# Decoder block on one core: a fixed order of three engines up to the first feature product, twelve warm products ahead of it, and a first weight chunk of four tiles

## The chip, the core and the metric

The kernel runs on one core of one Trainium2 chip. The metric is the device time of one execution in microseconds (us). The engines are PE (matrix products), DVE (VectorE), ACT (ScalarE), POOL (GpSimd) and SP, whose queue issues the loads.

## The reference, cut to what matters

One layer of a decoder runs on 256 prompt tokens and 8 x 4 sample tokens, 288 columns in all, with 2048 features. Its beginning is what the change touches:

```python
mod = silu(c) @ w_ada + b_ada                 # conditioning, 6 parts of 2048
sh1, sc1, g1, sh2, sc2, g2 = split(mod, 6)
h = rmsnorm(x, norm1) * (1 + sc1) + sh1       # modulated input
proj = h @ w_in                               # feature products
u_pool, z, xbc, dt_raw = split(proj, ...)
```

After it come the pooling mixer, the state-space mixer, the output projection, a gated feed-forward network and a last norm. All data is fp32, and the time is spent on products of weights that are streamed once from HBM.

## The kernel before, in words

The features lie on partitions: `xa` holds x as 16 blocks of 128 features by 288 columns. A **feature product** of fp32 accuracy is made of three PE products in the function `mm3` (lines 229 to 231): the weight is split into a rounded high half `whi` (a cast on ACT, L223) and a rest `wlo` (a subtraction on DVE, L224), the modulated input h likewise into `h1h` (ACT, L375) and `h1l` (DVE, L376), and PE adds whi\*h1h, whi\*h1l and wlo\*h1h.

The first projection (tiles called `xbc`) has 28 output tiles of 128 features. It doesn't wait for all of the conditioning: the 16 blocks of h are taken in six groups, `KGROUPS` = 1, 1, 2, 4, 4, 4 blocks. For each group, `ada_group_units` makes the conditioning of its blocks on PE (`adag`, L308), copies it out on ACT (`asb`, L263), turns it with a product (`adat`, L323), and adds the bias on DVE (`ada`, L333; `amul`, L275). `modulate` then makes h: a product with the reciprocal norm (L363), scale and shift of the prompt columns (L366), scale and shift of the sample columns (L372, L373), and the split (L375, L376). For group 0 the sample columns are done on DVE, for the others on POOL. Then `xbc_units` runs the 28 tiles of the group: group 0 copies its results from PSUM to SBUF alternately on ACT and DVE (L589), later groups add theirs on DVE (L591).

The weights come in pieces of 512 KB into 16 buffers (`raw`), issued by SP in the order of the program: four conditioning pieces of group 0, the chunks of group 0's weights, four conditioning pieces of group 1, and so on. `_xbc_chunks` cuts a group's weights into chunks of 1024 columns: in group 0, 8 tiles each and 4 in the last. There are two buffers each for `whi` and `wlo`. A planner orders the instructions of each engine by program order and by when it expects their inputs, so they needn't run in the order in which they are written.

The conditioning of later groups is mixed into the tiles of the group at hand: the generator `nxt` is pulled once after each tile listed in `AT` (for groups 0 and 1) or at the rate `AR` (from group 2). Four pulls load a batch of four pieces, and the next pull runs the products of this batch (in group 1's case also its modulation) and starts the next load. `AN` = 4 pulls are made ahead of group 0.

**Warm products** (`warm_pe`, L179) are 128 x 128 products whose result nobody reads. `WU` says how many: 14 at the start, 2 after each block of squares, 2 after each of the first two conditioning pieces, and 2 after group 0's `adat`.

The norm runs ahead of that: squares of x on ACT and DVE (L427, L429), their sums on PE (`ssum`, L431, and `ssum1b`, L191), a square root on ACT (L197), a reciprocal on DVE (L198), and a broadcast on PE (`pbrstd`, L202).

Of the kernel before, what the change touches and what calls it, by code (L numbers as in the profile page):

```python
# [36 lines left out]
EPS = 1e-6  # L37
WU = (14, 2, 2, 2, 2)
RAW0, RAW1, RAW2 = 8, 8, 1
# [5 lines left out]

AT = ([16, 18, 20, 22], [0, 1, 2, 3, 8, 10, 12, 18, 20, 22, 24, 26])
AR = (0, 0, 0.43, 0.62, 0.62)
# [89 lines left out]
def kernel(ctx: ExitStack, tc, ins, outs):  # L137
# [34 lines left out]
    nc.scalar.activation(sc_c[:, :, 0:NC9], ct, AF.Silu)  # L172

    wps = aux("warm")

# [17 lines left out]

    def rstd_of(ps, n, name, keep=True):
# [3 lines left out]
        nc.vector.reciprocal(r3, r3)  # L198
        pb = aux("pb" + name)
# [13 lines left out]
    def load(key):  # L213
# [3 lines left out]
        return t  # L217

    def split(raw, a, n, name, urgent=True):
        hi = wp[0].tile([P, RAWC], F32R, tag="whi", name="whi_" + name)  # L220
        lo = wp[0].tile([P, RAWC], F32R, tag="wlo", name="wlo_" + name)
        with tc.high_priority() if urgent else nullcontext():
            nc.scalar.copy(hi[:, :n], raw[:, a:a + n])  # L223
            nc.vector.tensor_tensor(lo[:, :n], raw[:, a:a + n], hi[:, :n].bitcast(F32), ALU.subtract)  # L224
        return hi, lo

# [33 lines left out]

    def ada_sb(ps, nb, name, r=P, pin=False):
        asb = kp.tile([P, 512], F32, tag="asb", name="asb_" + name)
        i = nc.scalar.copy(asb[0:r, :nb], ps[0:r, :nb])  # L263
        if pin:
            tc.keep_in_program_order(i)
        return asb
# [13 lines left out]
    def ada_group_units(gi):  # L280
# [7 lines left out]
        kstep = 2 if gk == 1 else 1  # L288
        begun = False
        first = True  # L290
        for q0 in range(0, nq, AQ[gi]):
            raws = []
            for q in range(q0, min(q0 + AQ[gi], nq)):
                raws.append((q, load(("ada", gi, q))))
                yield

            for q, raw in raws[::-1] if gi else raws:
                for kk in range(0, per, kstep):
                    k = q * per + kk
                    for j in range(nj if gk > 1 else 4):  # L300
                        if gk == 1:

                            ck, c = k + j // 2, kk * 256 + j * P
                        else:
                            ck, c = k, kk * nj * nb + j * nb
                        left = q0 + AQ[gi] >= nq and q == raws[0 if gi else -1][0] and kk + kstep >= per
                        with tc.high_priority() if begun else nullcontext():
                            i = nc.tensor.matmul(ps[32 * j:32 * j + 32, :nb], sc_c[:, ck, :], raw[:, c:c + nb],  # L308
                                                 start=first, stop=left, tile_position=(0, 32 * j))
                        if begun:  # L310
                            tc.keep_in_program_order(i)
                        begun = gi > 0
                    first = False
                if gi == 0 and q < WU[3]:
                    warm_pe(WU[2], raw[:, 0:P])
            begun = False
        r = 32 * nj
        if gi == 0:
            ready["xbc", 0, 0] = split(load(("xbc", 0, 0)), 0, RAWC, "xbc0_0")
        if gk == 1:  # L320
            asb = ada_sb(ps, nb, f"g{gi}", pin=gi == 0)
            pt = aux(f"adat_g{gi}")
            nc.tensor.matmul(pt[:, :r], asb[:, :nb], early[:, K_S2:K_S2 + r], start=True, stop=True)  # L323
            if gi == 0:
                warm_pe(WU[4], asb[:, 0:P])
        else:
            pt = ada_tr(ada_sb(ps, nb, f"g{gi}", r), nb, f"g{gi}", r)
# [30 lines left out]

    def modulate(xv, rstd, which, shp, k0, gk, name, eng=None):

        h = kp.tile([P, 4, N], F32, tag="hmod", name="h_" + name, bufs=2)
        hv = h[:, :gk, :]
        nc.vector.tensor_tensor(hv, xv,  # L363
                                rstd.unsqueeze(1).to_broadcast([P, gk, N]), ALU.mult)
        for i in range(gk):
            nc.vector.tensor_scalar(h[:, i, 0:NP], h[:, i, 0:NP], amul[:, which, k0 + i, 0:1],  # L366
                                    ada[:, shp, k0 + i, 0:1], ALU.mult, ALU.add)
# [4 lines left out]
        eng.tensor_tensor(hs, hs, sa, ALU.mult)  # L372
        eng.tensor_tensor(hs, hs, sb, ALU.add)  # L373
        for i in range(gk):
            nc.scalar.copy(xhi[0][k0 + i], h[:, i, :])  # L375
            nc.vector.tensor_tensor(xlo[0][k0 + i], h[:, i, :], xhi[0][k0 + i].bitcast(F32), ALU.subtract)  # L376
# [42 lines left out]


    nc.scalar.activation(warm, sc_c[:, 0, 0:1], AF.Sqrt, scale=0.0)
    warm_pe(WU[0])
    ssum = aux("ssum1")
    for q in range(4):
        sq = kp.tile([P, 4, N], F32, tag="hmod", name=f"sq{q}", bufs=2)
        if q % 2 == 0:
            nc.scalar.activation(sq, xa[q], AF.Square)  # L427
        else:
            nc.vector.tensor_tensor(sq, xa[q], xa[q], ALU.mult)  # L429
        for i in range(4):  # L430
            nc.tensor.matmul(ssum[32 * i:32 * i + 32, :N], ones[:, 0:32], sq[:, i, :],  # L431
                             start=(q == 0), stop=(q == 3), tile_position=(0, 32 * i))
        warm_pe(WU[1], sq[:, 0, 0:P])
    sqs = kp.tile([P, N], F32, tag="xsq", name="sqs", bufs=2)
    nc.vector.tensor_copy(sqs, ssum[:, :N])
    ssum = aux("ssum1b")
    col_sums(ssum, sqs, early[:, K_S4:K_S4 + 1], True, True)
    rstd1p, rstd1 = rstd_of(ssum, D, "rstd1")

# [879 lines left out]
```

## Time and profile before

| | |
|---|---|
| median of 3 runs | 1378.33 us (1378.28 to 1380.17) |
| profiled execution | 1378.2 us, of which its span (first to last instruction) 1376.3 us |
| PE busy in the span | 1354.7 us |
| DVE, ACT, POOL busy | 824.3, 570.2, 223.6 us |
| read from HBM | 309.78 MB |

The span is what the trace shows; 1.9 us of the execution lie around it. Times in the trace count from the span's start.

### The profile page before, as it was taken

The page shows a single profiled execution, that of the slowest core. Times are in us where ns is not written, and L with a number is a line of the kernel's source. Part 1 is how long each engine was busy: PE and PEld are TensorE (multiplying, and loading weights), DVE is VectorE, ACT ScalarE, POOL GpSimd, SP SyncE. Part 2 cuts the span into 40 slices and gives each one's busy share as a digit, 9 for nine tenths or more (in the row PEclk, how much of TensorE's full clock was granted, in tenths as well). Part 3 has the DMA queues.
Part 4 walks back from the last instruction along what each step waited for, and adds up shares of the span by engine and source line. Part 5 has one row for each costly group of instructions (what it writes and reads, how often), then busy time and mean ns, then how long its engine had stood idle before and what let it go on. Part 6 is the DMA issues. An engine that isn't in the chain of part 4 may idle for free.

```text
span 1376.3 us, 26243 instructions
## 1 busy us (share of the span) xinstructions
PE 1354.7 (98%) x10557; PEld 1254.3 (91%) x10557; DVE 824.3 (60%) x1376; ACT 570.2 (41%) x889; POOL 223.6 (16%) x430
## 2 busy tenths in 40 slices
PE   8999999999999999999999999999999999999997
PEld 7788987776779898989999999999999999999997
DVE  4875658977674348644665445666565556566553
ACT  4223224478553334533433333443433334443452
POOL 0000001212122213111221001212120012132221
PEclk9999999999999999999999999999999999999998
DMA  9987766988887878778555555555555555555531
GB/s 380 408 347 274 303 229 242 341 295 297 306 338 291 322 256 278 236 271 296 190 179 182 170 168 188 201 183 188 187 173 163 183 198 181 196 191 192 184 119 70
DMA packets 97194, 323.20 MB, mean 235 GB/s; under 512 B 10736, under 2 KB 19888, under 8 KB 97072
## 3 DMA queue, kind: packets, MB, share of 16 engines
q1 hardware_dynamic: 93168, 310.63, 63.8%
q0 software_dynamic: 3184, 9.69, 1.9%
q8 instruction: 83, 1.36, 0.4%
q10 hardware_dynamic: 720, 1.19, 0.2%
q14 instruction: 39, 0.32, 0.1%
HBM read 309.78 MB, written 10.39 MB: 233 GB/s over the span
## 4 chain that ended last, share of the span: by engine, by line
PE 94%; DVE 4%; DMA 1%; ACT 1%; issue 0%; POOL 0%; DVEq 0%; POOLq 0%; ACTq 0%
PE mm_down L231 7%; PE mm_down L229 7%; PE mm_down L230 7%; PE mm_gate L231 6%; PE mm_gate L229 6%; PE mm_val L230 6%; PE mm_gate L230 6%; PE mm_val L231 6%; PE mm_val L229 6%; PE adap L258 4%; PE xbc L229 4%; PE xbc L231 4%; PE xbc L230 4%; PE mm_out L229 3%; PE mm_out L230 2%; PE mm_out L231 2%
## 5 line engine op out<-in xcount | busy, mean ns | idle before, releaser
L229 PE MATMUL mm_down<-ah,whi_down 128*128 128x288 f32 x688 | 203.7, 296 | 0.0
L231 PE MATMUL mm_down<-ah,wlo_down 128*128 128x288 f32 x688 | 203.5, 296 | 0.0
L230 PE MATMUL mm_down<-al,whi_down 128*128 128x288 f32 x688 | 203.3, 295 | 0.0
L231 PE MATMUL mm_gate<-h2h,wlo_gate 128*128 128x288 f32 x640 | 190.2, 297 | 0.0
L229 PE MATMUL mm_gate<-h2h,whi_gate 128*128 128x288 f32 x640 | 189.8, 297 | 0.0
L230 PE MATMUL mm_gate<-h2l,whi_gate 128*128 128x288 f32 x640 | 189.3, 296 | 0.0
L230 PE MATMUL mm_val<-h2l,whi_val 128*128 128x288 f32 x640 | 188.8, 295 | 0.0
L231 PE MATMUL mm_val<-h2h,wlo_val 128*128 128x288 f32 x640 | 188.5, 295 | 0.0
L229 PE MATMUL mm_val<-h2h,whi_val 128*128 128x288 f32 x640 | 188.0, 294 | 0.0
L224 DVE TENSOR_TENSOR wlo_gate<-raw_gate,whi_gate 128x1024 fp32r<-128x1024 f32 x80 | 98.0, 1226 | 139.1 <-ACT whi_gate L223 139.0
L224 DVE TENSOR_TENSOR wlo_down<-raw_down,whi_down 128x1024 fp32r<-128x1024 f32 x96 | 107.5, 1120 | 116.7 <-ACT whi_down L223 115.2
L223 ACT CAST whi_down<-raw_down 128x1024 fp32r<-128x1024 f32 x96 | 92.2, 961 | 168.9 <-PE mm_down L230 120.6
L223 ACT CAST whi_gate<-raw_gate 128x1024 fp32r<-128x1024 f32 x80 | 83.9, 1050 | 163.7 <-PE mm_gate L230 71.8
L229 PE MATMUL xbc<-h1h,whi_xbc 128*128 128x288 f32 x448 | 136.0, 305 | 4.3 <-ACT h1h L375 2.3
L223 ACT CAST whi_val<-raw_val 128x1024 fp32r<-128x1024 f32 x80 | 84.1, 1051 | 123.9 <-issue 100.2
L231 PE MATMUL xbc<-h1h,wlo_xbc 128*128 128x288 f32 x448 | 131.5, 301 | 2.2 <-DVE wlo_xbc L224 2.0
L230 PE MATMUL xbc<-h1l,whi_xbc 128*128 128x288 f32 x448 | 132.7, 297 | 0.0
L230 PEld LDWEIGHTS mm_down<-al,whi_down 128*128 128x128 f32 x688 | 129.7, 189 | 0.0
L231 PEld LDWEIGHTS mm_down<-ah,wlo_down 128*128 128x128 f32 x688 | 129.6, 188 | 0.0
L229 PEld LDWEIGHTS mm_down<-ah,whi_down 128*128 128x128 f32 x688 | 129.6, 188 | 0.0
L229 PEld LDWEIGHTS mm_gate<-h2h,whi_gate 128*128 128x128 f32 x640 | 120.4, 188 | 5.0 <-ACT ah L1084 3.4
L230 PEld LDWEIGHTS mm_gate<-h2l,whi_gate 128*128 128x128 f32 x640 | 120.7, 189 | 0.0
(324 smaller groups left out, 2989.6 us busy)
## 6 DMA issues: line engine op xcount, KB each, us to landing
raw_adap<-wflat SPq DMA_DIRECT2D x128, 512.0 KB, 5.7
raw_gate<-wflat SPq DMA_DIRECT2D x80, 512.0 KB, 3.6
raw_val<-wflat SPq DMA_DIRECT2D x80, 512.0 KB, 3.6
raw_ada<-wflat SPq DMA_DIRECT2D x64, 512.0 KB, 9.0
raw_xbc<-wflat SPq DMA_DIRECT2D x55, 512.0 KB, 7.2
raw_down<-wflat SPq DMA_DIRECT2D x48, 512.0 KB, 3.5
raw_out<-wflat SPq DMA_DIRECT2D x32, 512.0 KB, 6.9
raw_down<-wflat SPq DMA_DIRECT2D x32, 384.0 KB, 2.9
```

What stands on the lines that cost most here:

```text
L223: nc.scalar.copy(hi[:, :n], raw[:, a:a + n])
L224: nc.vector.tensor_tensor(lo[:, :n], raw[:, a:a + n], hi[:, :n].bitcast(F32), ALU.subtract)
L229: nc.tensor.matmul(ps, whi[:, w], bh, start=first, stop=False)
L230: nc.tensor.matmul(ps, whi[:, w], bl, start=False, stop=False)
L231: nc.tensor.matmul(ps, wlo[:, w], bh, start=False, stop=last)
L258: nc.tensor.matmul(ps[32 * j:32 * j + 32, :nb], sc_c[:, k, :], raw[:, c:c + nb], start=(k == 0), stop=(k == KT - 1), tile_position=(0, 32 ...
```

## The change

Everything from the first warm products to the modulation of group 0 is written inside a block `in_order`, which chains the instructions of PE, ACT and DVE so that each engine runs its own in the order in which they are written. To write that order by hand, the helpers become generators that stop at given places: `ada_group_units` for group 0 (loads; products of piece 0, 1, 2, 3; copy, `adat` and warm products; bias), `modulate_steps` (norm product; scale and shift; split) and `split_steps` (cast; subtraction).

The order is: squares and their sums; conditioning piece 0; column sums; piece 1; square root and reciprocal; piece 2; broadcast; norm product; piece 3; `asb`, `adat` and the warm products; bias and scale; casts of the first two weight chunks on ACT; scale and shift of h on DVE; subtraction for chunk 0; split of h; subtraction for chunk 1.

The warm products after the conditioning pieces are gone, and those after `adat` are 12 instead of 2. Group 0's chunks now hold 4, 8, 8 and 8 tiles instead of 8, 8, 8 and 4. Chunks 2 and 3 are loaded directly behind group 1's first four pieces. The pulls in `AT` move.

```diff
-WU = (14, 2, 2, 2, 2)
+WU = (14, 2, 2, 2, 12)
-AT = ([16, 18, 20, 22], [0, 1, 2, 3, 8, 10, 12, 18, 20, 22, 24, 26])
+AT = ([12, 14, 16, 18], [1, 2, 8, 9, 16, 17, 18, 19, 24, 25, 26, 27])
...
-    return [(list(range(k0, k0 + gk)), list(range(m, min(m + mper, ET)))) for m in range(0, ET, mper)]
+    cuts = [0, *range(mper // 2 if gi == 0 else mper, ET, mper), ET]
+    return [(list(range(k0, k0 + gk)), list(range(a, b))) for a, b in zip(cuts, cuts[1:])]
...
+    @contextmanager
+    def in_order(*engines):
+
+        traced = nc.cur_bb.bb.instructions
+        n0 = len(traced)
+        yield
+        prev = {}
+        for i in list(traced[n0:]):
+            if i.engine in engines:
+                if i.engine in prev:
+                    tc.add_manual_dep(i, prev[i.engine].name, mybir.DependencyInfo(
+                        mybir.DependencyClass.NoSync, mybir.DependencyReason.DATA), reason="in_order")
+                prev[i.engine] = i
...
+    def split_steps(raw, a, n, name):
+        hi = wp[0].tile([P, RAWC], F32R, tag="whi", name="whi_" + name)
+        yield nc.scalar.copy(hi[:, :n], raw[:, a:a + n])
+        lo = wp[0].tile([P, RAWC], F32R, tag="wlo", name="wlo_" + name)
+        nc.vector.tensor_tensor(lo[:, :n], raw[:, a:a + n], hi[:, :n].bitcast(F32), ALU.subtract)
+        yield hi, lo
...
-                if gi == 0 and q < WU[3]:
-                    warm_pe(WU[2], raw[:, 0:P])
...
-        if gi == 0:
-            ready["xbc", 0, 0] = split(load(("xbc", 0, 0)), 0, RAWC, "xbc0_0")
...
-    drain(ada_group_units(0))
-    for ci in range(1, 2):
-        ready["xbc", 0, ci] = load(("xbc", 0, ci))
-    modulate(xav(0, KGROUPS[0][1]), rstd1p, 0, 0, 0, KGROUPS[0][1], "g0", nc.vector)
+    with in_order(*(e.engine for e in (nc.tensor, nc.scalar, nc.vector))):
...
+        cond = ada_group_units(0)
+        next(cond)
+        first = [load(("xbc", 0, ci)) for ci in range(2)]
+        sqs = kp.tile([P, N], F32, tag="xsq", name="sqs", bufs=2)
+        nc.vector.tensor_copy(sqs, ssum[:, :N])
+        next(cond)
+        ssum = aux("ssum1b")
+        col_sums(ssum, sqs, early[:, K_S4:K_S4 + 1], True, True)
+        next(cond)
+        rstd1p, rstd1 = rstd_of(ssum, D, "rstd1", mid=lambda: next(cond))
+        mod = modulate_steps(xav(0, KGROUPS[0][1]), rstd1p, 0, 0, 0, KGROUPS[0][1], "g0", nc.vector)
+        next(mod)
+        next(cond)
+        next(cond)
+        drain(cond)
+        parts = [split_steps(t, 0, len(ms) * P, f"xbc0_{i}") for i, (t, (_, ms)) in
+                 enumerate(zip(first, _xbc_chunks(0)))]
+        for p in parts:
+            next(p)
+        next(mod)
+        ready["xbc", 0, 0] = next(parts[0])
+        drain(mod)
+        ready["xbc", 0, 1] = next(parts[1])
...
     for _ in range(AN):
         next(nxt)
+    for ci in (2, 3):
+        ready["xbc", 0, ci] = load(("xbc", 0, ci))
```

## Rows read from the trace of the kernel before

**Rows 1.** The page's busy line: busy us, share of the span, instructions.
```profile
PE 1354.7 (98%) x10557; PEld 1254.3 (91%) x10557; DVE 824.3 (60%) x1376; ACT 570.2 (41%) x889; POOL 223.6 (16%) x430
```

**Rows 2.** Busy time by stretch: length, engines, PEclk, DMA share, GB/s.
```profile
22.80:26.20 3.40, 3.40 (x17) 3.39 (x16) 1.47 (x4) 1.21 (x3) 0.00 (x0) 0.51 1.03 411
26.20:29.60 3.40, 3.40 (x26) 3.29 (x25) 1.78 (x5) 2.25 (x5) 0.00 (x0) 0.99 1.03 405
29.60:39.40 9.80, 9.71 (x171) 8.87 (x170) 8.01 (x16) 5.10 (x13) 0.49 (x2) 1.00 1.03 408
39.40:62.40 23.00, 20.95 (x220) 16.18 (x220) 18.74 (x40) 5.58 (x8) 0.60 (x2) 1.00 1.03 407
62.40:95.00 32.60, 30.80 (x270) 26.19 (x271) 24.52 (x49) 8.94 (x12) 0.95 (x2) 1.00 0.89 343
95.00:250.00 155.00, 154.74 (x1254) 134.55 (x1253) 101.41 (x200) 52.56 (x68) 9.15 (x24) 1.00 0.75 277
```

**Rows 3.** The chain that ended last, 12.5 to 22 us: start, us, what.
```profile
14.59 0.42 PE warm L179 x2
...
15.60 0.30 PE warm L179 x2
...
16.48 0.64 PE warm L179 x4
17.12 1.05 PE adag L308 x32
...
18.52 0.45 PE adat_g L323 x2
...
19.74 1.22 DVE wlo_xbc L224
...
21.32 0.44 ACT h1h L375
...
21.80 0.40 PE xbc L229
```

**Rows 4.** Instructions in order of time: start, us, engine, line, what.
```profile
1.06 5.63 PE L179 MATMUL warm<-ones 128*128 128x128 f32 x28 [1.06 <-DVE ones L162]
...
18.79 0.66 PE L179 MATMUL warm<-asb_g,ones 128*128 128x128 f32 x4
...
19.41 0.41 DVE L366 TENSOR_SCALAR h_g<-h_g,amul,ada 128x256 f32<-128x256 f32 x1
...
20.88 0.18 DVE L372 TENSOR_TENSOR h_g<-h_g,amul 128x32 f32<-128x32 f32 x1
...
29.65 1.96 PE L308 MATMUL adag<-raw_ada,sc_c 128*32 128x128 f32 x64
```

**Rows 5.** PE's groups from 21.8 to 29.65 us: count, busy us, mean ns, idle before.
```profile
L229 PE MATMUL xbc<-h1h,whi_xbc 128*128 128x288 f32 x15 | 4.9, 348 | 2.3 <-ACT h1h L375 2.3
```

**Rows 6.** Weight pieces: SP's issues with their time to landing, and casts on ACT.
```profile
L216 SPq DMA_DIRECT2D raw_ada<-wflat x2: 443/464/484, 4.4 to 4.9; - x2
DMA to landing us min/median/max: 9.3/9.6/10.0
...
L216 SPq DMA_DIRECT2D raw_xbc<-wflat x1: 328/328/328, 13.6 to 13.6; - x1
DMA to landing us min/median/max: 11.1/11.1/11.1
...
L216 SPq DMA_DIRECT2D raw_xbc<-wflat x2: 328/328/328, 20.9 to 22.3; - x2
DMA to landing us min/median/max: 9.6/9.6/9.6
...
L223 ACT CAST whi_xbc<-raw_xbc x7: 622/1049/1054, 28.4 to 56.3; 128x1024 fp32r<-128x1024 f32 x5, 128x512 fp32r<-128x512 f32 x2
```

**Rows 7.** PE's waits from 39.4 to 62.4 us: total, times, longest.
```profile
PE xbc L229 <- DVE cvp L591: 1.4, 4, 0.4
PE xbc L231 <- DVE wlo_xbc L224: 0.6, 1, 0.6
```

More of the change, by code (lines that the diff above doesn't have):

```diff
@@ L1 @@
-from contextlib import ExitStack, nullcontext
+from contextlib import ExitStack, contextmanager, nullcontext
 import numpy as np
@@ L192, in col_sums, with rstd_of @@
                              skip_group_check=True)
-    def rstd_of(ps, n, name, keep=True):
+    def rstd_of(ps, n, name, keep=True, mid=None):
         r3 = kp.tile([P, 3], F32, tag="r3", name="r3" + name)
@@ L198, in rstd_of @@
         nc.vector.reciprocal(r3, r3)
+        if mid:
+            mid()
         pb = aux("pb" + name)
@@ L217, in load @@
         return t
+    def split_steps(raw, a, n, name):
[4 more added lines that the diff above has]
+        yield hi, lo
     def split(raw, a, n, name, urgent=True):
-        hi = wp[0].tile([P, RAWC], F32R, tag="whi", name="whi_" + name)
-        lo = wp[0].tile([P, RAWC], F32R, tag="wlo", name="wlo_" + name)
         with tc.high_priority() if urgent else nullcontext():
-            nc.scalar.copy(hi[:, :n], raw[:, a:a + n])
-            nc.vector.tensor_tensor(lo[:, :n], raw[:, a:a + n], hi[:, :n].bitcast(F32), ALU.subtract)
-        return hi, lo
+            _, parts = split_steps(raw, a, n, name)
+        return parts
     def mm3(ps, whi, wlo, c, bh, bl, first, last, n=P):
@@ L259, in ada_mm, with ada_sb @@
                              start=(k == 0), stop=(k == KT - 1), tile_position=(0, 32 * j))
-    def ada_sb(ps, nb, name, r=P, pin=False):
+    def ada_sb(ps, nb, name, r=P):
         asb = kp.tile([P, 512], F32, tag="asb", name="asb_" + name)
-        i = nc.scalar.copy(asb[0:r, :nb], ps[0:r, :nb])
-        if pin:
-            tc.keep_in_program_order(i)
+        nc.scalar.copy(asb[0:r, :nb], ps[0:r, :nb])
         return asb
@@ L288, in ada_group_units @@
         kstep = 2 if gk == 1 else 1
-        begun = False
-        first = True
         for q0 in range(0, nq, AQ[gi]):
@@ L294, in ada_group_units @@
                 raws.append((q, load(("ada", gi, q))))
[L295 to L313, printed above, removed]
-                if gi == 0 and q < WU[3]:
-                    warm_pe(WU[2], raw[:, 0:P])
@@ L316, in ada_group_units @@
-            begun = False
+                if gi:
+                    yield
+            order = [(q, raw, kk) for q, raw in (raws[::-1] if gi else raws) for kk in range(0, per, kstep)]
+            for n, (q, raw, kk) in enumerate(order):
+                if gi == 0 and kk == 0:
+                    yield
+                k = q * per + kk
+                for j in range(nj if gk > 1 else 4):
+                    if gk == 1:
+                        ck, c = k + j // 2, kk * 256 + j * P
+                    else:
+                        ck, c = k, kk * nj * nb + j * nb
+                    begun = gi > 0 and n + j > 0
+                    with tc.high_priority() if begun else nullcontext():
+                        i = nc.tensor.matmul(ps[32 * j:32 * j + 32, :nb], sc_c[:, ck, :], raw[:, c:c + nb],
+                                             start=q0 + n == 0, stop=q0 + AQ[gi] >= nq and n + 1 == len(order),
+                                             tile_position=(0, 32 * j))
+                    if begun:
+                        tc.keep_in_program_order(i)
@@ L317, in ada_group_units @@
         r = 32 * nj
         if gi == 0:
-            ready["xbc", 0, 0] = split(load(("xbc", 0, 0)), 0, RAWC, "xbc0_0")
+            yield
         if gk == 1:
-            asb = ada_sb(ps, nb, f"g{gi}", pin=gi == 0)
+            asb = ada_sb(ps, nb, f"g{gi}")
             pt = aux(f"adat_g{gi}")
@@ L325, in ada_group_units @@
                 warm_pe(WU[4], asb[:, 0:P])
+                yield
         else:
@@ L357, in samp, with modulate, modulate_steps @@
         return ap.rearrange("p (b l) -> p b l", b=NB)
-    def modulate(xv, rstd, which, shp, k0, gk, name, eng=None):
+    def modulate(*args):
+        for _ in modulate_steps(*args):
+            pass
+    def modulate_steps(xv, rstd, which, shp, k0, gk, name, eng=None):
         h = kp.tile([P, 4, N], F32, tag="hmod", name="h_" + name, bufs=2)
@@ L364, in modulate @@
                                 rstd.unsqueeze(1).to_broadcast([P, gk, N]), ALU.mult)
+        yield
         for i in range(gk):
@@ L373, in modulate @@
         eng.tensor_tensor(hs, hs, sb, ALU.add)
+        yield
         for i in range(gk):
@@ L417, in xav @@
         return xa[k0 // 4][:, k0 % 4:k0 % 4 + gk, :]
[L421 to L438, printed above, removed]
     w0_ctx = ExitStack()
@@ L854 @@
     adas = chain(*(ada_part_units(p, AY) for p in (2, 3, 4)))
-    drain(ada_group_units(0))
-    for ci in range(1, 2):
-        ready["xbc", 0, ci] = load(("xbc", 0, ci))
-    modulate(xav(0, KGROUPS[0][1]), rstd1p, 0, 0, 0, KGROUPS[0][1], "g0", nc.vector)
+    with in_order(*(e.engine for e in (nc.tensor, nc.scalar, nc.vector))):
+        nc.scalar.activation(warm, sc_c[:, 0, 0:1], AF.Sqrt, scale=0.0)
+        warm_pe(WU[0])
+        ssum = aux("ssum1")
+        for q in range(4):
+            sq = kp.tile([P, 4, N], F32, tag="hmod", name=f"sq{q}", bufs=2)
+            if q % 2 == 0:
+                nc.scalar.activation(sq, xa[q], AF.Square)
+            else:
+                nc.vector.tensor_tensor(sq, xa[q], xa[q], ALU.mult)
+            for i in range(4):
+                nc.tensor.matmul(ssum[32 * i:32 * i + 32, :N], ones[:, 0:32], sq[:, i, :],
+                                 start=(q == 0), stop=(q == 3), tile_position=(0, 32 * i))
+            warm_pe(WU[1], sq[:, 0, 0:P])
+        cond = ada_group_units(0)
[21 more added lines that the diff above has]
+        ready["xbc", 0, 1] = next(parts[1])
     def next_groups():
```

## The prediction

> **What bounds the kernel now.** I read first the page's busy line: PE works 1354.7 of 1376.3 us [rows 1], so only time in which PE stands, or runs at half clock, can be won. Next the table of stretches, to find that time [rows 2]: from 95 to 250 us PE is idle 0.3 of 155, so a lead that PE has at 95 us stays a lead. Ahead of 95 us there are three losses to see. PE stands before the first feature product. From 22.8 to 26.2 the granted clock is 0.51, that is 1.2 GHz instead of 2.4, and PE starts 17 products where the next, equally long stretch has 26 [rows 2]. And from 39.4 to 95 PE is idle 2.05 + 1.80 us [rows 2]; in the first of these two stretches it waits for DVE [rows 7]. Then the chain of waits up to the first feature product [rows 3], instruction by instruction [rows 4]. The weight stream stands at a DMA share of 1.03 and 407 to 411 GB/s up to 62.4 [rows 2], which looks like the bound. Whether it is, landings decide [rows 6], not the share.
>
> What the chain says: PE is through with group 0's conditioning at 18.17, `adat` starts at 18.52, DVE then makes bias and scale, and at 19.41 to 19.82 the prompt columns. The sample columns start only at 20.88, because the 1.22 us subtraction of a weight chunk was put between [rows 3, 4]. `h1h` runs 21.32 to 21.76, and the first feature product starts at 21.80, after PE stood for 2.3 us [rows 3, 5]. One us later the clock falls.
>
> **Term 1: the start of the first feature product.** (a) PE's way to `adat`. Three pieces of the chain are warm products that go away: 0.42, 0.30 and 0.64, in sum 1.36 us [rows 3]. The rest of PE's work there stays and is only put in another order. `adat` would start at 18.52 - 1.36 = 17.16. From below: the eight records at 0.10 each (half of 5.63/28 = 0.20, the pace of the first warm products, which ran slower than later ones [rows 4]) are 0.8; from above I allow 1.6, if the order also closes small stalls. The last conditioning piece lands at 4.9 + 10.0 = 14.9 [rows 6], so it doesn't limit this.
>
> (b) From `adat` to h1h. Now it is 21.76 - 18.52 = 3.24 us. The subtraction that stood between the two scale steps moves behind them, which saves 20.88 - 19.82 = 1.06: h1h is there 2.2 us after `adat`. ACT must run the casts of both chunks in front of h1h, 0.62 and 1.05 [rows 6]; it is free when `asb` ends, so it is through 1.7 us after `adat`, just when h is ready. The chunks follow the last conditioning piece, which lands at 14.9 [rows 6]: 256 KB and 512 KB at 410 GB/s [rows 2] are 0.64 and 1.28 us, so they are there at 15.5 and 16.8, before `asb` ends, and neither cast waits for data.
>
> (c) The twelve warm products are 24 records on PE, behind `adat`'s 0.27 (18.52 to 18.79 [rows 3, 4]) and in front of the first feature product. One record is at least 0.10 (above) and at most 0.66/4 = 0.165, which includes the tail of the last [rows 4]. I take 0.11, near the lower end since the tail counts once: 2.7 us, with ends 2.4 and 4.0. So PE is free 3.0 us after `adat` and h1h has been there for 0.8: the warm products themselves set the start, at 17.16 + 3.0 = 20.15. **-1.65 us**, ends -2.2 (16.9 + 2.67 = 19.6) and +0.2 (17.7 + 4.3). Behind it nothing is late: the subtraction of chunk 0 is half as long as before and ends with h1l about 2.9 after `adat`, and that of chunk 1 (1.22) at 4.2, while PE asks for it after four tiles at 3.0 + 1.6.
>
> **Term 2: the clock.** The stretch 22.8 to 26.2 lost 3.4 x 0.49 = 1.67 us [rows 2]. Before it PE had stood for 2.3 us. In the new order the longest stand is that for `asb`, about 0.35 (18.17 to 18.52 now), and the warm products close the rest. **-1.7 us**, ends -1.7 and 0.
>
> A rule of the Trainium skill is weighed here. The page "TensorE: Matmul & The Clock Gate", in its section on the warmup mystery, says that the gate watches the engine by a clock of its own, which the kernel's start doesn't set, so that the same kernel sees its clock change at different products from run to run. The trace shows a fall that comes 1.0 us after PE took up work again, which fits. By this rule some executions of before may have lost less than 1.7, and the median would gain less; if none of it is gained, the sum is -2.2. Rival B comes to nearly the same by another way.
>
> **Term 3: the conditioning in between.** The pulls move: group 1's batch from tile 16 to 12 of group 0, group 2's two batches to tiles 1 and 16 of group 1 and group 3's first to 24. PE's work stays the same. One batch (64 records, 1.96 us [rows 4]) that PE now does before 39.4, where it waits for nothing (9.71 busy of 9.80), lands in group 1, where PE stands 2.05 of 23 us [rows 2]. The upper bound is that it fills all of it: -1.95. But 1.4 of the 2.05 is waits for DVE's adds [rows 7], and DVE is busy 18.7 of 23 there, so a product batch fills a gap only where it is ready at that moment.
>
> Against it: PE comes nearer to the weights. Chunk 2 of group 0 lands at 13.6 + 11.1 = 24.7 [rows 6], now 0.64 earlier, 24.1. Cast and subtraction (1.05 and 1.22 [rows 3, 6]) end at 26.4. PE gets to tile 12 at 20.15 + 12 x 0.39 = 24.8 (0.39 is three products at 3.40/26 [rows 2]). That would be a wait of 1.6, if group 1's batch (1.96) weren't pulled just there; it covers the wait. In the same way group 1's first chunk lands at 22.3 + 9.6 = 31.9, is split by 34.2, and PE gets there at 20.15 + 28 x 0.39 + 1.96 = 33.0, with the batch at tile 1 as cover. Without cover: +1.6 and +1.2, of which the second shrinks by the first. I take **-0.5**, a quarter of the bound, ends -1.95 and +1.6.
>
> **At nothing:** the loads. Their bytes and count are the same, and before group 1's first chunk stand the same bytes as now. SP issues chunk 3 ahead of group 2's first batch instead of behind it, so that the last piece of this batch lands where chunk 3 lands now, at 20.9 + 9.6 = 30.5 [rows 6]; it is used from tile 1 of group 1 on, after 33.0. If that cover were gone (PE 2.5 us earlier than I think), each piece that is late would cost what it is late. The `in_order` chain and the generators issue no instruction of their own. The stalls from 62.4 on I leave as they are.
>
> **Sum:** -1.65 - 1.7 - 0.5 = -3.85. The span goes from 1376.3 to 1372.4; with the 1.9 us around it 1374.3, against 1378.2 of the profiled execution. The median of the runs is 0.1 above that execution: I say 1374.4 us, -0.28%. A change within 0.2% (2.8 us) can't be told from none here.
>
> **Rivals.**
>
> A. The weight stream is the bound, and a lead of PE is waited off. For it: a share of 1.03 at 410 GB/s for over 50 us [rows 2]. Against it: PE has no wait for a landing among those from 39.4 to 62.4 [rows 7], and group 0's chunk 2 lies in its buffer for 3.7 us before its cast (24.7 to 28.4 [rows 6]). But a split needs 2.3 us after each landing, and after the change group 1's first chunk has only 33.0 - 31.9 = 1.1. If the batches don't cover, 1.6 at tile 12 and some 0.7 in group 1 come off the lead, and term 3 wins nothing: -1.65 - 1.7 + 1.6 + 0.7 = -1.05, 1377.3 us. Carried to its end, every gain of PE is waited off at some later landing, and the time stays at 1378.3. The page "Perfetto Trace Analysis" of the Trainium skill, section "Identifying the Most-Contended Engine", says that gains come as a rule from the engine with the highest use; with the DMA taken as that engine, it speaks for this end.
>
> B. The clock falls all the same, at another place. For it: it fell with a delay, after PE was at work again [rows 2, 3], so the stands at `asb` and tile 12 might do it too. Against it: the gaps of up to 0.6 from 39.4 to 62.4 were followed by no fall, the clock is 1.00 there [rows 2, 7]. Term 2 is then 0: -2.15, 1376.2 us.
>
> C. Slower than before: each wait at a chunk lets the clock fall. PE, run close behind the landings, stands 1.6 us at tile 12, and again at chunks of group 1; each fall costs 1.7 [rows 2]. One fall makes -3.35 + 1.6 + 1.7 = 0; it decides from the third on: -3.35 + 1.6 + 3 x 1.7 = +3.35, 1381.7 us. Against it: a stand of 1.6 is shorter than the 2.3 that was followed by a fall, and PE's gaps of up to 0.6 from 39.4 to 62.4 [rows 7] left the clock at 1.00.
>
> **How the numbers follow.** Forecast 0.64 (own range 1372.4 to 1375.6), A 0.15, B 0.09, C 0.07; 0.05 is left for a plan of the later parts, made anew, that costs or wins some 2 us. The best ends, -2.2 - 1.7 - 1.95 = -5.85, give 1372.4, and 0.2 of that plan 1372.2; upwards the range takes in B and A to 1378.2. Outside are C, A's last tenths and most of the plan's share. Faster by over 0.2% (below 1375.6): the forecast, 0.64. Slower by over 0.2% (above 1381.1): C and a bit of the plan's share, 0.08. Within: A, B and the rest, 0.28.
>
> **What would show it.** In the profile of the changed kernel: `adat` near 17.2; the 24 warm records without a gap for 2.7 us; the first feature product near 20.15, with h1h done before it (if h1h ends later than the warm products, term 1b is wrong); granted clock 1.00 from 20 to 30; 28 tiles and one batch later group 1 begins at 33 to 33.5; PE's lead at the start of group 2 about 4 us, and as much at 95 us. Wrong it would be by a PE wait for `wlo_xbc` at tile 12 or 28, by PEclk below 1 in any stretch after 20 us, or by a lead that is there at 33 us and gone at 62.

## The result and the profile after

The changed kernel takes 1380.7 us (median of 22 runs, 1379.85 to 1383.72) against 1378.55 for the kernel before (22 runs on the same chip): ratio 1.0017, 95% interval 1.0010 to 1.0023. It is 0.17% slower, where 1374.4 was forecast, and outside the range of 1372.2 to 1378.2. The profiled execution took 1381.8 us, of which the span is 1380.0.

The beginning went as forecast. The next lines are from the instructions in order of time, on PE and on ACT (start, us, engine, line, what); they answer to [rows 3, 4].

```profile
17.10 0.43 PE L339 MATMUL adat_g<-early,asb_g 128*128 128x64 f32 x2 [0.38 <-ACT asb_g L284]
17.37 2.90 PE L194 MATMUL warm<-asb_g,ones 128*128 128x128 f32 x24
20.02 0.64 PE L250 MATMUL xbc<-h1h,whi_xbc 128*128 128x288 f32 x3
...
18.76 0.43 ACT L398 CAST h1h<-h_g 128x288 fp32r<-128x288 f32 x1 [0.25 <-DVE h_g L395]
```

`adat` starts at 17.10 (forecast 17.16), the 24 warm records run without a gap, h1h is done at 19.19, and the first feature product starts at 20.02 (forecast 20.15; before, 21.80). The table of stretches of the changed kernel answers to [rows 2], with the same columns:

```profile
22.80:26.20 3.40, 3.31 (x40) 2.91 (x42) 2.12 (x5) 1.85 (x5) 0.00 (x0) 1.00 1.03 412
26.20:29.60 3.40, 3.25 (x67) 2.66 (x55) 2.31 (x6) 2.14 (x5) 0.48 (x2) 1.00 1.03 407
29.60:39.40 9.80, 8.85 (x106) 7.48 (x107) 7.08 (x12) 4.95 (x11) 1.03 (x1) 1.00 1.02 408
39.40:62.40 23.00, 22.11 (x239) 18.62 (x239) 20.56 (x43) 5.41 (x8) 0.62 (x2) 1.00 1.03 407
62.40:95.00 32.60, 30.68 (x270) 26.24 (x270) 24.31 (x49) 9.18 (x13) 0.95 (x2) 1.00 0.97 384
95.00:250.00 155.00, 154.72 (x1236) 133.80 (x1235) 99.63 (x199) 52.16 (x69) 9.05 (x24) 0.99 0.72 270
```

The clock stays at 1.00 where it had fallen to 0.51, and from 39.4 to 62.4 PE is idle 0.89 us instead of 2.05. New is the idle time of 0.95 us from 29.6 to 39.4. And the last line holds what decides: from 95 to 250 us PE is busy as long as before (154.72 against 154.74 us), yet it starts 1236 products instead of 1254.

To follow a lead through the span, take the n-th PE product of each kind in both traces and subtract the start times. Worked out so (median over the products within 0.6 us of the time named; minus means that the changed kernel is ahead):

| time in the kernel before, us | 22 | 27 | 34 | 68 | 99 | 228 | 250 | 395 | 512 | 700 | 1100 | 1300 |
|---|---|---|---|---|---|---|---|---|---|---|---|---|
| changed minus before, us | -1.80 | -2.73 | -0.96 | -2.96 | -2.89 | -2.00 | -0.38 | -0.14 | +0.65 | +1.49 | +2.72 | +3.66 |

So a lead of about 3 us is there at 68 us, and then it melts for the rest of the span. One step of it, 1.5 us from 231 to 236, is a fall of the clock that this execution had (below). The other 5.05 us (3.66 + 2.89 - 1.5) come bit by bit, and not from waits: behind 95 us PE's waits add up to 3.4 us before and 3.3 after. In place of a gain of 3.9, then: -2.9 + 5.05 = +2.15 us. The medians differ by 2.15 too; that it agrees to the hundredth is chance, as the runs of either kernel spread over more than 3 us.

The slow loss shows in the number of products in a stretch without waits. The same stretch of the kernel before, and then of the changed kernel (length, PE, PEld, DVE, ACT, POOL busy and instructions, clock, DMA):

```profile
1000.00:1300.00 300.00, 300.00 (x2255) 300.00 (x2254) 173.40 (x255) 118.22 (x166) 54.78 (x107) 1.00 0.56 187
```

```profile
1000.00:1300.00 300.00, 300.00 (x2247) 300.00 (x2246) 175.02 (x257) 117.98 (x166) 54.61 (x106) 1.00 0.55 185
```

At the same clock PE gets through 2247 instead of 2255 products. The page's groups of costly instructions say which (busy us, mean ns of one), before. `mm_gate` and `mm_val` are the two products of the feed-forward network that read its modulated input h2:

```profile
L229 PE MATMUL mm_gate<-h2h,whi_gate 128*128 128x288 f32 x640 | 189.8, 297 | 0.0
L230 PE MATMUL mm_val<-h2l,whi_val 128*128 128x288 f32 x640 | 188.8, 295 | 0.0
```

and after:

```profile
L251 PE MATMUL mm_val<-h2l,whi_val 128*128 128x288 f32 x640 | 191.3, 299 | 0.0
L250 PE MATMUL mm_gate<-h2h,whi_gate 128*128 128x288 f32 x640 | 189.9, 297 | 0.0
```

One product lasts longer than the time to the next, since they overlap in the trace. From start to start of neighbouring products (worked out from the trace; the mean of `xbc` moves by up to 0.2 ns with the gaps that are counted), `mm_val` goes from 132.3 to 134.0 ns, `xbc` from 132.3 to 133.5, and `mm_out`, the output projection, from 132.5 to 133.6. Times their number behind 99 us (1920, 968 and 768) that is 3.3, 1.2 and 0.8 us, together 5.3: about the whole of the slow loss. `mm_gate` (133.4 and 133.3) and `mm_down`, the last product of the network (133.05 both times), stay. `mm_down` doesn't read the h tiles; the others do.

### The profile page after: what moved, and what is told of

It reads as the page before. It is cut to its first block, busy times and chain, and to the rows that moved or that the text cites. A ratio compares the mean times of both kernels' runs of the same rounds, so it can differ in the third digit from the quotient of the medians.

```text
span 1380.0 us, 26263 instructions
## 1 busy us (share of the span) xinstructions
PE 1360.7 (99%) x10569; PEld 1260.0 (91%) x10569; DVE 822.8 (60%) x1376; ACT 570.1 (41%) x889; POOL 224.4 (16%) x430
## 4 chain that ended last, share of the span: by engine, by line
PE 94%; DVE 4%; ACT 1%; issue 1%; POOL 0%; DMA 0%; DVEq 0%; POOLq 0%; ACTq 0%
PE mm_down L250 7%; PE mm_down L252 7%; PE mm_down L251 7%; PE mm_gate L250 6%; PE mm_val L251 6%; PE mm_val L252 6%; PE mm_val L250 6%; PE mm_gate L252 6%; PE mm_gate L251 6%; PE adap L279 4%; PE xbc L252 4%; PE xbc L250 4%; PE xbc L251 4%; PE mm_out L250 3%; PE mm_out L251 3%; PE mm_out L252 2%
## 5 line engine op out<-in xcount | busy, mean ns | idle before, releaser
L252 PE MATMUL xbc<-h1h,wlo_xbc 128*128 128x288 f32 x448 | 132.1, 302 | 2.6 <-DVE wlo_xbc L240 2.5
L250 PEld LDWEIGHTS mm_val<-h2h,whi_val 128*128 128x128 f32 x640 | 120.9, 189 | 0.0
```

The costliest lines, as they stand in the source:

```text
L250: nc.tensor.matmul(ps, whi[:, w], bh, start=first, stop=False)
L252: nc.tensor.matmul(ps, wlo[:, w], bh, start=False, stop=last)
```

## The experiments

**Where the loss comes from.** The change writes the squares and the norm in the block `in_order`, which stands much further down in the kernel function. The call `new_operand("h1")`, which names the 32 h tiles, stayed at its place and so now comes ahead of the first use of the tags `hmod`, `xsq`, `r3` and `rstd`. Addresses in SBUF are given out in the order in which tags are first named: the h tiles lie 12704 B lower, `h1h` at 22656 instead of 35360. Modulo 128 that is 0 instead of 32; the weight buffers stay. The products of h2 use the same tiles. Theory 1: the place of h sets the pace. Theory 2: the order of instructions does. The first four kernels part them.

`a_lay`, the changed kernel with the four tags named first, so that h lies where it lay before:

```diff
+    for tag, shape, n in (("hmod", [P, 4 * N], 2), ("xsq", [P, N], 2), ("r3", [P, 3], 1), ("rstd", [P, N], 1)):
+        nc.gpsimd.memset(kp.tile(shape, F32, tag=tag, name="first_" + tag, bufs=n)[:, 0:1], 0.0)
```

> The changed kernel, with four tags of its first pool named before the operand tiles h, so that every tile of h lies where the kernel before has it (the first at byte 35360 of a partition instead of 22656). Four tiny POOL fills are added. Theory 1 (place): PE's products that read h are slower in the changed kernel because of where h lies. Then their pace goes back (mm_val near 132.3 ns a product, xbc near 132.4 after 100 us) and the time is 4 to 5 us below the changed kernel: 1375.6 to 1376.8, faster than before. Theory 2 (order): the later slowness comes from the new order of instructions. Then nothing changes: 1380 to 1381.5, mm_val at 134.

`b_lay`, the kernel before with h where the change puts it (the three tiles named with it keep what lies behind h at the changed kernel's places):

```diff
+    new_operand("h1")
+    etb = kp.tile([P, NB, NH], F32, name="etb")
+    ssq = kp.tile([P, N], F32, tag="ssx", name="ssq")
+    sbx = kp.tile([P, P + G6], F32, name="sbx")
     nc.scalar.activation(warm, sc_c[:, 0, 0:1], AF.Sqrt, scale=0.0)
```

> The kernel before, with the tiles of h named first, so that they lie where the changed kernel has them (the first at byte 22656). No instruction is added or moved. Theory 1 (place): PE's pace on products that read h falls to that of the changed kernel, and the time rises by 4 to 5 us: 1382.5 to 1383.5. Theory 2 (order): 1378.5, as before.

`a_h32` and `a_h64`, the changed kernel with h 32 and 64 B further on (for `a_h64`; `a_h32` has 8 and 24):

```diff
+    nc.gpsimd.memset(kp.tile([P, 16], F32, name="gap1"), 0.0)
     new_operand("h1")
+    nc.gpsimd.memset(kp.tile([P, 16], F32, name="gap2"), 0.0)
```

> The changed kernel with 32 bytes put ahead of h and 96 behind it: h moves by 32 bytes, everything behind it by 128. Theory 1a (place modulo 64 bytes): h then lies at 32 modulo 64 as in the kernel before, and the time falls by 4 to 5 us, 1375.6 to 1376.8. Theory 1b (the place as a whole, such as its distance from the weights): no or another change. Theory 2 (order): 1380 to 1381.5.

> The control of the run with 32 bytes: the changed kernel with 64 bytes ahead of h and 64 behind it, so that the place modulo 64 stays 0. Theory 1a: no change, 1380 to 1381.5. Theory 1b, in the form that the remainder by 128 counts: another time. Theory 2: 1380 to 1381.5.

Measured, each against the kernel before on the same chip (1378.83): `a_lay` 1375.65 us (ratio 0.9980, 0.9971 to 0.9989), `b_lay` 1385.04 (1.0043, 1.0030 to 1.0055), `a_h32` 1377.05 (0.9988, 0.9979 to 0.9997), `a_h64` 1373.37 (0.9964, 0.9951 to 0.9976). Theory 1 holds and theory 2 falls: with h at its old place the changed kernel is faster than the one before, and the kernel before becomes slower with h at the new one. In `a_lay` the lead is -2.5 us at 68, still -2.5 at 228, and after the clock's fall at 231 stays at -0.99 from 250 us to the end. `b_lay` rises by 6.2 us where 4 to 5 were expected; its trace loses 7.05 us from 99 to 1300 us, 1.5 of them in a fall of the clock near 234. That 64 B further on is fastest refutes the form in which the place was to count modulo 64, though `a_h32` alone (1377.05, expected 1375.6 to 1376.8) would nearly have fitted it.

The stretch from 1000 to 1300 us of `a_lay`, and then of `a_h64`:

```profile
1000.00:1300.00 300.00, 300.00 (x2255) 300.00 (x2254) 174.12 (x252) 117.79 (x165) 53.74 (x106) 1.00 0.59 186
```

```profile
1000.00:1300.00 300.00, 300.00 (x2261) 300.00 (x2260) 172.93 (x251) 118.04 (x166) 53.46 (x105) 1.00 0.58 185
```

**Place, or distance from the weights?** `a_h128` puts h a whole 128 B further on (`gap1` of 32 elements, no `gap2`). The weight buffers lie in two pools: `xbc` and `mm_val` read their weights from the first, `mm_gate` from the second. `w_64` leaves h where the change puts it and moves the buffers of the first pool instead:

```diff
+    wpad = ctx.enter_context(tc.tile_pool(name="wpad", bufs=1, side="right"))
+    nc.gpsimd.memset(wpad.tile([P, 16], F32, name="gapw"), 0.0)
     wp[0].add(ctx.enter_context(tc.tile_pool(name="w1", bufs=1, side="right")), RAW1, SPLIT1)
```

> The changed kernel with h a whole 128 B further on (22784) and all that lies behind it as in the kernel where h lies 64 B further on (22720, 1373.4 us). If the place counts by its rest modulo 128, as the four places seen so far leave open (0: 1380.7, 32: 1377.1 and 1375.7, 64: 1373.4), it is as slow as the changed kernel, 1380.7, with 134 ns from product to product for mm_val. Rival, the place counts by more than that rest, or what lies behind h made the gain: 1373 to 1377.

> The changed kernel with h where the change puts it (22656) and the weight buffers of the first pool 64 B lower (212896 instead of 212960), so that h and these weights lie to each other as they do, modulo 128, where h is 64 B further on. Theory 1b, only the distance of h and the weights counts: xbc, uz, mm_val and half of mm_out, which read these weights, go as fast as there (mm_val 132.2 instead of 134.0 ns from product to product), mm_gate, whose weights stay, stays at 133.6: about 7.3 us x 0.6 less than the changed kernel, 1376. Theory 1c, the address of h by itself counts: no change, 1380.7. Anything between: both count.

Measured: `a_h128` 1381.18 us (ratio 1.0016, 1.0007 to 1.0024), `w_64` 1375.59 (0.9979, 0.9971 to 0.9988). A shift by 128 B changes nothing, and moving the weights alone speeds up the products that read them; 1376 was expected for that. Groups of `w_64`:

```profile
L250 PE MATMUL mm_gate<-h2h,whi_gate 128*128 128x288 f32 x640 | 189.9, 297 | 0.0
L251 PE MATMUL mm_val<-h2l,whi_val 128*128 128x288 f32 x640 | 186.6, 292 | 0.0
```

`mm_val` drops from 299 to 292 ns; `mm_gate`, whose weights lie in the second pool and were not moved, stays at 297. Put together by the distance of weights and h (weights minus h, modulo 128 B), the mean spacing of products in ns:

| kernel | first pool: distance | xbc | mm_val | second pool: distance | mm_gate |
|---|---|---|---|---|---|
| before, `a_lay` | 64 | 132.3 | 132.3 | 96 | 133.4 |
| `a_h32` | 64 | 132.5 | 132.3 | 96 | 134.1 |
| `a_h64` | 32 | 132.6 | 132.3 | 64 | 132.2 |
| `w_64` | 32 | 132.6 | 132.1 | 0 | 133.3 |
| after, `b_lay` | 96 | 133.5 | 134.0 | 0 | 133.3 |
| `a_h128` | 96 | 133.4 | 134.4 | 0 | 133.2 |

Distances of 32 and 64 give 132.1 to 132.6, those of 96 and 0 give 133.2 to 134.4, in both pools. Neither address sorts them by itself: with h at 0 the products are slow for weights at 96 and at 0 and fast for weights at 32. Other distances were not run, and what in the chip does this no run here shows.

**The change at a place held fixed.** `b_h64` is `b_lay` with the two gaps of `a_h64`, so the kernel before with h at 22720.

> The kernel before the change with h at the address that is fastest in the changed kernel (22720, 64 modulo 128). Theory 1 (the address of h sets the pace of the products that read it, in any order): the kernel before at 22656 took 1385.0, the changed kernel wins 1380.7 - 1373.4 = 7.3 us from 22656 to 22720, so 1377.7 here, and the distance between the two kernels at this address is 4.3 us. Rival (the address pays only with the order of the changed kernel): 1381 to 1385.

It took 1376.23 us (ratio 0.9980, 0.9971 to 0.9989), 1.5 less than expected. With h at the same place in both kernels:

| h at (modulo 128) | kernel before | changed kernel | difference |
|---|---|---|---|
| 35360 (32) | 1378.8 | 1375.65 (`a_lay`) | -3.2 |
| 22656 (0) | 1385.0 (`b_lay`) | 1380.7 | -4.3 |
| 22720 (64) | 1376.2 (`b_h64`) | 1373.4 (`a_h64`) | -2.9 |

So the order, the warm products, the chunks and the pulls are worth 2.9 to 4.3 us. That this is near the 3.85 of the forecast is in part luck, as the terms came out otherwise (below). Part of it is the clock. The four traces with a mean granted clock of 0.998 have no fall between 10 us and the last 10 us of the span, the ten others (0.993 to 0.997) have one or two. Among executions at 0.998 the kernel before took 1377.0 to 1377.4 us (five of 72) and `a_lay` 1375.2 to 1375.4 (three of 11), which leaves 2.0 of the 3.2 us at this place.

**Which part brings it.** The base is now `a_h64` (1373.4). `c_at` takes back the lists of pulls; `b_at` gives them to `b_h64`:

```diff
-AT = ([12, 14, 16, 18], [1, 2, 8, 9, 16, 17, 18, 19, 24, 25, 26, 27])
+AT = ([16, 18, 20, 22], [0, 1, 2, 3, 8, 10, 12, 18, 20, 22, 24, 26])
```

> The changed kernel with h 64 B further on (1373.4 us) as the base, and the lists of the pulls as they were before the change (group 1's batch at tile 16 of group 0, and so on). Term 3 of the prediction as forecast: the moved pulls are worth 0.5 us, so without them 1373.9. Rival, the batches are cover for the chunks (the uncovered waits of term 3, 1.6 and 0.7): PE waits for the subtraction of chunk 2 at tile 12, 1375 to 1375.7. Second rival, the trace of the changed kernel has ACT stand behind POOL for group 1's first cast while group 0's sums wait for their copies; with the pull four tiles later this stand only comes later: 1373.4, no change.

> The kernel before with h at 22720 (1376.2 us) and the lists of pulls of the changed kernel: term 3 without terms 1 and 2. In the changed order the lists were worth 1378.2 - 1373.4 = 4.8 us (2.3 to 3.1 us of lead at 68 us in the traces), where 0.5 was forecast. If the lists win that by themselves: 1372 to 1373.5. If they win it only where PE starts early, since they decide whether an early start is kept or waited off: 1375.7 to 1376.2, that is the 0.5 of term 3 or nothing.

`c_at` took 1378.19 us (ratio 0.9994, 0.9985 to 1.0003), `b_at` 1376.18 (0.9976, 0.9967 to 0.9985). `c_at` lies above all three times expected; `b_at` has the time of its second reading, but not for its reason, as will be seen. The medians also hold falls of the clock at 231 us, which some executions have and others not. The traces up to 68 us are free of those; the three with the old start hold the fall at 23 us:

| us | first product of group 0 | of group 1 | of group 2 | lead at 68 us |
|---|---|---|---|---|
| before | 21.80 | 39.38 | 60.54 | |
| old start, old lists (`b_h64`) | 22.19 | 40.00 | 61.14 | +0.61 |
| old start, new lists (`b_at`) | 22.75 | 41.68 | 59.75 | -1.20 |
| new start, old lists (`c_at`) | 20.47 | 39.78 | 61.17 | +0.64 |
| new start, new lists (`a_h64`) | 20.54 | 39.31 | 58.46 | -2.50 |

With the old lists the early start and the steady clock leave nothing: 2.3 us of lead at 27 us are gone at the start of group 1. The lists are worth 1.8 us with the old start and 3.1 with the new one, where 0.5 was forecast.

The differences of the columns say where. Group 1 takes 21.1 to 21.4 us with the old lists and 18.1 to 19.1 with the new ones, with either start. Group 0 takes 17.6 to 18.9 us with the old start, with the fall of the clock in it, and 18.8 to 19.3 with the new start, without one. Without the 1.7 us of the fall the kernel before would need 15.9, so 2.9 us of what terms 1 and 2 win are lost again in group 0. PE's waits there in the changed kernel that the trace names are two for copies from PSUM:

```profile
PE xbc L250 <- ACT cvp L593: 0.9, 2, 0.7
```

That is about a third of the 2.9; the rest these rows don't name. And no batch of conditioning products moves from group 0 to group 1: in all five traces two stand ahead of group 1's first product and three behind it. The second and the third of them, before and then after:

```profile
35.55 1.95 PE L308 MATMUL adag<-raw_ada,sc_c 128*32 128x128 f32 x64
...
42.81 1.95 PE L308 MATMUL adag<-raw_ada,sc_c 128*32 128x128 f32 x64
```

```profile
36.91 1.95 PE L328 MATMUL adag<-raw_ada,sc_c 128*32 128x128 f32 x64
...
44.89 1.95 PE L328 MATMUL adag<-raw_ada,sc_c 128*32 128x128 f32 x64
```

The median of `b_at` shows nothing of what the lists win, because its executions differ in the clock: seven of 11 have a mean of 0.993 to 0.995 and took 1376.0 to 1378.1 us, four have 0.996 to 0.998 and took 1372.7 to 1374.5. The profiled one is of the first kind; the clock falls at the start and once more behind 228 us:

```profile
22.80:26.20 3.40, 3.40 (x15) 3.34 (x16) 2.00 (x4) 0.80 (x2) 0.00 (x0) 0.55 1.03 410
...
228.00:250.00 22.00, 21.77 (x136) 15.05 (x135) 15.46 (x38) 9.16 (x15) 3.44 (x9) 0.84 0.60 226
```

`a_h64` has four of five executions at 0.997 or more, 1373.1 to 1374.1 us. So it may be that at a steady clock the lists alone bring it all, and that the early start with its warm products is worth what it saves of falls. The executions at 0.998 speak for it: `b_at` took 1373.2 (one), `a_h64` 1373.4 and 1374.1. The 1.3 us between the two traces at 68 us are also no more than what the fall at 23 us costs (1.7 in the kernel before). With so few executions it stays open. What the old lists cost is seen in `c_at`: PE's waits from 39.4 to 62.4 us, and DVE in order of time.

```profile
PE xbc L250 <- DVE cvp L597: 1.4, 4, 0.4
```

```profile
46.82 0.45 DVE L597 TENSOR_TENSOR cvp<-cvp,xbc 128x288 f32<-128x288 f32 x1 [0.25 <-PE xbc L252]
47.20 0.73 DVE L388 TENSOR_SCALAR h_g<-h_g,amul,ada 128x256 f32<-128x256 f32 x2
47.84 0.45 DVE L597 TENSOR_TENSOR cvp<-cvp,xbc 128x288 f32<-128x288 f32 x1
48.20 0.82 DVE L399 TENSOR_TENSOR h1l<-h_g,h1h 128x288 fp32r<-128x288 f32 x2
```

Group 2's scale and split stand between the adds, and PE waits four times for an add: the 1.4 us of [rows 7]. With the new lists these instructions come later, and the changed kernel has one wait there, from the same view of waits:

```profile
PE xbc L252 <- DVE wlo_xbc L240: 0.7, 1, 0.7
```

From 20 to 68 us PE is idle 4.0 us in `c_at` and 2.4 in `a_h64`. That is 1.6 of the 3.1 us; the rest is not seen as idle time.

**ACT behind POOL.** In the changed kernel PE starts no product between 30.45 and 31.44 us. POOL, DVE, ACT and PE in order of time:

```profile
29.52 1.11 POOL L395 TENSOR_TENSOR h_g<-h_g,ada 128x32 f32<-128x32 f32 x1
...
29.26 1.27 DVE L240 TENSOR_TENSOR wlo_xbc<-raw_xbc,whi_xbc 128x1024 fp32r<-128x1024 f32 x1
...
30.66 0.43 ACT L398 CAST h1h<-h_g 128x288 fp32r<-128x288 f32 x1 [0.73 <-POOL h_g L395]
31.00 0.39 ACT L593 COPY cvp<-xbc 128x288 f32<-128x288 f32 x1
...
31.44 0.41 PE L250 MATMUL xbc<-h1h,whi_xbc 128*128 128x288 f32 x1 [0.70 <-ACT cvp L593]
```

POOL's 32 columns take 1.11 us and end 0.10 after DVE's subtraction; the same instruction took 0.24 in the kernel before, beside a copy from PSUM and DVE's scale and shift of the prompt columns. This agrees with the Trainium skill, page "SBUF — State Buffer", section "SBUF: two separate sides", by which POOL and DVE share one pair of ports that one instruction holds to its end. ACT waits for POOL with group 1's cast, a copy from PSUM stands behind it, and PE waits for that copy. `c_dve` gives these columns to DVE:

```diff
-            modulate(xav(k0, gk), rstd1, 0, 0, k0, gk, f"g{gi}")
+            modulate(xav(k0, gk), rstd1, 0, 0, k0, gk, f"g{gi}", nc.vector if gi == 1 else None)
```

> The same base (1373.4 us) with the sample columns of group 1's h on VectorE instead of POOL. Theory: in the changed kernel ACT waits for POOL's sample columns with its cast of h, and the copies of group 0's sums stand queued behind, which stops PE by 0.39 and 0.86 us between 28.7 and 31.5 us; without it PE's lead over the kernel before at 34 us grows by 0.8 to 1.2 us, and as PE is the bound from there on, 1372.4. Rival: VectorE, which also adds the sums and subtracts the chunks, passes the delay on, 1373.4 or up to 1 us more.

It took 1372.94 us (ratio 0.9962, 0.9949 to 0.9974), between the two times expected. At 34 us, where the lead was to grow by 0.8 to 1.2, it is 0.08 smaller than that of `a_h64`, and group 0 takes 18.76 us instead of 18.77: the wait is passed on, and PE still waits 0.7 us for ACT's copies there. At 68 us the lead is 0.26 larger. The median can't be told from that of `a_h64`. So ACT's wait for POOL is not what makes group 0 long.

**The warm products.** `c_wu` has two instead of twelve, `c_wu8` eight (on `c_dve`), by the last number of `WU`.

> The same base (1373.4 us) with two warm products instead of twelve in front of the first feature product. Terms 1c and 2 as forecast: h1h then sets the first product, at about 19.2 instead of 20.0 us, PE stands about 1.3 us before it and the granted clock falls soon after, which costs the 1.7 us of the fall in the kernel before: 1373.4 - 0.8 + 1.7 = 1374.3. Rival, the stand is too short for a fall, or the fall comes anyhow at another place: 1372.6. Second rival, an earlier start runs into the weights of chunk 2 and is waited off: 1373.4 without a fall, 1375.1 with one.

> The changed kernel with h at 22720, group 1's sample columns on VectorE (1372.9 us) and eight warm products instead of twelve. PE is then through with them 0.9 us earlier, at about 19.15, where h1h ends (19.2). Theory, PE's own work sets the time behind it and no stand is left for the clock to fall: 1372.1, the first feature product at 19.2. Rival, the early start is waited off at the copies and the subtractions of groups 0 and 1: 1372.9. Second rival, the short stand is enough for a fall: 1374.5.

`c_wu` took 1375.17 us (ratio 0.9969, 0.9959 to 0.9980). Its profiled execution in order of time, ACT and then PE, and two stretches of its table:

```profile
19.25 1.04 ACT L238 CAST whi_xbc<-raw_xbc 128x1024 fp32r<-128x1024 f32 x1 [1.37 <-DMA raw_xbc<-wflat]
20.20 0.43 ACT L398 CAST h1h<-h_g 128x288 fp32r<-128x288 f32 x1
...
20.68 0.40 PE L250 MATMUL xbc<-h1h,whi_xbc 128*128 128x288 f32 x1 [2.33 <-ACT h1h L398]
```

```profile
20.00:22.80 2.80, 2.12 (x11) 2.06 (x12) 2.05 (x3) 1.03 (x4) 0.00 (x0) 0.76 1.03 410
22.80:26.20 3.40, 3.31 (x17) 2.96 (x17) 1.92 (x4) 1.19 (x3) 0.00 (x0) 0.69 1.03 411
```

In this execution the second chunk landed late (19.2 us, against 16.8 in the changed kernel), and in the fixed order h1h stands behind its cast. PE stood 2.33 us and the clock fell, which cost 2.8 x 0.24 + 3.4 x 0.31 = 1.73 us. So the expected early start at 19.2 didn't happen here, and what a stand of 1.3 us does isn't shown. The median is that of the second rival (1375.1), but it didn't come about in that rival's way, by a wait for chunk 2. The same late landing is in the trace of `a_h32`, with twelve warm products:

```profile
18.88 1.04 ACT L238 CAST whi_xbc<-raw_xbc 128x1024 fp32r<-128x1024 f32 x1 [1.22 <-DMA raw_xbc<-wflat]
19.84 0.43 ACT L398 CAST h1h<-h_g 128x288 fp32r<-128x288 f32 x1
```

There PE was at its warm products until h1h was done, began group 0 at 20.31, and its clock didn't fall: what the warm products cover is also a late landing. Three of the seven executions of `c_wu`, at a clock of 0.997, took 1372.3 to 1373.9. `c_wu8` took 1372.18 (ratio 0.9951, 0.9939 to 0.9963), the fastest of all, as expected to 0.1:

```profile
17.32 2.00 PE L194 MATMUL warm<-asb_g,ones 128*128 128x128 f32 x16
19.20 0.67 PE L250 MATMUL xbc<-h1h,whi_xbc 128*128 128x288 f32 x3
...
18.71 0.43 ACT L398 CAST h1h<-h_g 128x288 fp32r<-128x288 f32 x1 [0.26 <-DVE h_g L395]
```

The warm products end when h1h does, PE doesn't stand, and the lead over `c_dve` is 1.4 us at 22 and 1.3 at 68. Of that 0.7 comes from `adat`, which starts at 17.05 in this execution and at 17.72 in that of `c_dve`; the medians differ by 0.76. The earlier start is kept: group 0 takes 18.88 us, about as long as in `c_dve` (18.76).

## Why the prediction was wrong

**The step that failed** is the paragraph "At nothing", and with it the sentence that a lead which PE has at 95 us stays a lead. It asked which instructions the new generators issue (none) and not in which order the tiles are named, so it left out that the moved block shifts h in SBUF. That is a term of +5.05 us on the products that read h, and `a_lay` takes it out: 1375.65, inside the stated range and 1.25 above the 1374.4. The bound of 2 us for "a plan of the later parts, made anew" was the nearest to it, but the plan of the later parts is the same; the same instructions take longer.

**Term 1** was right: 20.02 for 20.15, with h1h 0.8 us ahead of the end of the warm products. The closeness is in part luck of the execution: in the eight traces with the new start and twelve warm products, the first product starts between 19.93 and 20.70. That neither cast waits for data failed in two of the ten traces with the new start (1.22 us in `a_h32`, 1.37 in `c_wu`). **Term 2** was right in its mechanism: the clock is 1.00 from 20 to 30 us. It fell near 23 us in all four traces with the old start and in none of the nine with the new start and eight or twelve warm products.

**Term 3** was wrong in its mechanism and its size, and terms 1 and 2 were taken as independent of it. It counted on a batch that moves from group 0 into group 1 and fills a gap there; no batch moves. What the lists change is where the batches, and DVE's work behind them, stand within group 1, and that is worth 1.8 to 3.1 us where 0.5 was forecast. In group 0 the forecast left out that PE doesn't keep its pace: the lead of 2.7 us at 27 is 0.96 at 34, and group 1 started at 38.8, where 33 to 33.5 was forecast. That number also left out the second batch, which PE ran ahead of group 1 in both kernels. Without the new lists `c_at` keeps nothing of terms 1 and 2; with them 2.50 stays, which against `b_h64` (+0.61) is 3.1: 1.8 from the lists (to `b_at`) and 1.3 from the start and the clock (to `a_h64`). The forecast of about 4 us at the start of group 2 was 2.6 (57.96 for 60.54).

**Rival A** had a part of it, a lead of PE that is lost again, but not its way: not at landings, with the sum of 1377.3. With the old lists the lead does go as A says, since group 1 begins at 39.4 to 40.0 us with either start; with the new lists it doesn't, since `c_wu8` keeps its earlier start. The wait for `wlo` that it names is there once in group 1, 0.7 us. **Rival B**, a fall at another place, is not there up to 228 us. The fall behind it came in some executions of nearly every order; the trace of `b_lay`, which has the order of before, has one (near 234) and that of `a_h64` hasn't, so the change doesn't bring it. **Rival C**, which gave a slower kernel, had the sign right and the cause wrong: in the changed kernel no stand at a chunk made the clock fall.

## What to carry to other kernels

Where a change moves code that names tiles, compare the addresses of the operands of the long product runs before and after, and price the spacing of their products, not only waits and instruction counts. A stretch in which an engine is busy as long but starts fewer instructions is the sign of it. And a lead is a gain only if what comes behind it keeps the pace: here an early start without the new lists gave nothing, so such parts are to be priced together.

## What the runs showed of the hardware

The same products, at the same clock and without waits, take 132.1 to 134.4 ns from start to start, by the distance of the weights and h in SBUF modulo 128 B, at the four distances that were run; over one kernel that was 7.3 us (1380.7 to 1373.4 for 64 B). The page "SBUF — State Buffer" of the Trainium skill, section "A bandwidth-pool intuition that's wrong (but worth ruling out)", gives PE a second, independent read port for the weights. That section says nothing of addresses, and by it one would not look for such a dependence; the measurement shows one.

The clock fell at 231 us in some executions and not in others, with the same order of instructions: in the changed kernel's profiled execution

```profile
231.10:234.50 3.40, 3.40 (x18) 1.85 (x22) 2.69 (x6) 2.59 (x7) 0.34 (x1) 0.52 0.00 0
```

which costs 3.4 x 0.48 = 1.6 us (1.5 by the table of leads), and not in that of `a_h64`. PE is not idle before it (busy 3.10 of the 3.10 us from 228.0); it runs small products of the state-space mixer among the others. The runs of `a_h64` took 1373.1 us at a mean clock of 0.997 and 1375.9 at 0.995. This fits the rule of the Trainium skill that the prediction weighed (page "TensorE: Matmul & The Clock Gate", section on the warmup mystery), by which the same kernel sees its clock change at different products from run to run.
